# A two-layer diffusion block in split fp32: one modulation unit on VectorE, hi and lo side by side in layer 1, the last norm's shift as two columns

## The chip, the cores and the metric

The kernel runs on one core of one Trainium2 chip. The metric is the device time in microseconds of one execution, the median over runs.

## What is computed

256 context tokens and 256 tokens of x, 1024 channels each, pass through two layers; the result is the final norm of the x tokens. Each layer has a mixer (layer 0 an mLSTM in two directions, layer 1 attention over a neighbourhood and the context) and a convolutional feed-forward. Both are wrapped in a norm that is scaled and shifted, and gated, by a modulation computed from a vector (c for x, c_ctx for the context):

```python
mod_x = jnp.split((silu_c @ ada_w[i] + ada_b[i])[:, None, :], 6, axis=-1)
hx = modulate(rmsnorm(xx, norm1_g[i]), mod_x[0], mod_x[1])
yc, yx = mlstm_mixer(...)          # layer 0
yc, yx = na_mixer(...)             # layer 1, x only
xx = xx + mod_x[2] * yx
hx = modulate(rmsnorm(xx, norm2_g[i]), mod_x[3], mod_x[4])
xx = xx + mod_x[5] * conv_ffn(hx, ...)
# layer 0: the same for the context, with mod_c

def conv_ffn(h, w_up, b_up, conv_w, conv_b, w_down, b_down):
    u = dwconv(h @ w_up + b_up, conv_w, conv_b)
    a, g = jnp.split(u, 2, axis=-1)
    return (a * jax.nn.silu(g)) @ w_down + b_down
```

FF_HIDDEN is 2816, so the up product has 44 tiles of 128 rows, 22 for a and 22 for g; the down product takes 22 hidden tiles.

## The kernel before

**Numbers.** All large products keep fp32 accuracy with three matmuls of a faster kind: `split` and `split_w` (line 480s) write hi (a cast on ScalarE) and lo (the rest, a subtraction on VectorE) of a tile, and `mm3` adds hi x hi, hi x lo and lo x hi into one PSUM bank. Where one stream of 256 tokens is the moving operand (layer 1's feed-forward, the attention's output), `two_parts` already places hi and lo in the two halves of one page of 128x512.

**Storage.** 62 pages of 128x512, eight half pages, three raw weight buffers of 128x1024, five buffers each for the weights' hi and lo, eight PSUM banks.

**Order.** No engine's order is written out. The functions record operations into a `Plan`; its `run` schedules the list once, with a cost for each operation, into one fixed sequence for each engine. Among the operations that could start on an engine it takes the one that is due first. An operation is due when its earliest TensorE user needs it, with TensorE's own recorded order as the clock (`nominal`), but at most `LATE` (1,000,000 ns, so in effect never) after its nominal time. All instructions are issued from one line of `run`, L141; the profile therefore tells them apart by tile names.

**Modulation.** Twelve units (layer, u), u = 0 to 5: u = 0, 1 and 3, 4 hold halves of shift and scale of the two norms, u = 2 and 5 the two gates. (0, 0) and (0, 1) come first in a special form. The others are emitted one step at a time by `trickle()`, called after tiles of the main work; `ada_need` finishes a unit where it is needed. `ada_tensor` (tiles `ra`, `ada`, `adat`) does a unit with 2 x 32 small matmuls and two transposes. `ada_vector` does it on VectorE: for each of eight row blocks m it loads two pages, and one `scalar_tensor_tensor` per page and stream multiplies by the row `crow` and sums along it (written to `aj` for the context's stream and over `ra` itself for x's). `ADA_VECTOR` lists the units done so: (0, 4) and all of layer 1. Layer 1's later units are needed for x alone.

```python
ADA_VECTOR = [(0, 4)] + [(1, u) for u in range(6)]
```

**The feed-forward of layer 0** (`feed_forward(0)`, 512 tokens) goes in three groups of hidden tiles (8, 8, 6): all up tiles of the group, then eight down tiles `dn` (weights `rdn`, `hdn`, `ldn`), each followed by `residual`. In the first group ScalarE first copies the bank to a half page `rb` with the bias, and VectorE adds gate x `rb` to the token page `xr`. Gate 2, unit (0, 5), is due just ahead of these. An up tile (`up`, in `ffn_up`) is 8 x `mm3`; ScalarE then reads the bank twice, once for `fu` (with bias) and once for `fc`; VectorE adds the two outer taps to `fc`; ScalarE makes `sg`, VectorE the product `pr`, and `split` the hidden pair (`hhid`, `lhid`, or `bhid` side by side in layer 1).

**Layer 1** after its attention: `no`, eight output tiles from the pages `boS`, each with `residual` (through `rb`) and `norm_add`. Then `last_feed_forward` on x's 256 tokens: up tiles of j and, four tiles behind (`LAG`), the down products of an earlier j, into four banks. The first up tiles don't wait for the norm: `Early` multiplies the tokens by the norm's scale (`etn`), splits them (`ben`), and starts the products of four up tiles `ms` from them, with weights `ren21up` loaded in half pages by `paged_w`; the norm's factor comes in afterwards, as `mup` = bank x `rsn`. The shift's part of these four tiles is made apart by `shift_terms`: 32 small fp32 matmuls `wsn<-ren21up,shn` on TensorE, a copy `wssn`, a transpose, a copy `wsen`. `norm_end` makes the factor: `rbn<-ones,sqn`, `msn`, a power on GpSimd `rsn`, the diagonals `dhn` and `dln`, `rbn<-dhn`. The remaining tiles use the normed pages `bhn`.

Of the kernel before, what the change touches and what calls it, by code (L numbers as in the profile page):

```python
# [9 lines left out]
F32 = mybir.dt.float32  # L10
# [48 lines left out]
ADA_VECTOR = [(0, 4)] + [(1, u) for u in range(6)]  # L59
# [3 lines left out]
class Plan:  # L63
# [13 lines left out]
    SWITCH = 1300  # L77
    PATIENCE = 2500
# [8 lines left out]
    def __init__(self, nc, tc):  # L87
# [7 lines left out]
        self.slow = set()  # L95
        self.ops_engine = []
# [87 lines left out]
    def add(self, engine, cost, ins, outs, fns, table, dma=False):  # L184
# [30 lines left out]
        self.ops.append(dict(i=i, e=engine, frees=any(x.space == bass.MemoryType.PSUM for x in ins), window=self.AHEAD_LOAD if load else self.AHEAD_PAGE if takes else self.AHEAD, cost=cost, deps=deps, tiles=tiles, fns=fns, table=table,  # L215
# [3 lines left out]
    def run(self):  # L219
# [17 lines left out]
        for o in reversed(ops):  # L237
# [6 lines left out]
            due[o["i"]] = min(t, nominal[o["i"]] + self.LATE)  # L244
# [159 lines left out]
def diffusion_block(ctx: ExitStack, tc: tile.TileContext, I: dict, out: bass.AP):  # L404
# [92 lines left out]

    def two_parts(name, n):
# [112 lines left out]
    def ada_vector(l, u):  # L611
# [100 lines left out]
    def shift_terms(name, raw, shift, streams):  # L712
# [15 lines left out]
        return e  # L728

# [477 lines left out]
    def ffn_up(l, streams, early, ms, h):  # L1207
# [7 lines left out]
        def up(j, part):  # L1215
# [15 lines left out]
            else:  # L1231
                ps = bank(f"up{l}{m}")
                W = split_w(I["ff_up"][l, m], f"up{l}{m}")
                for k in range(KD):
                    mm3(ps[:, :n], cut(W, P * k, P * k + P), cut(h[k], 0, n), k == 0, k == KD - 1)
                nc.scalar.activation(out=u[:, :n], in_=ps[:, :n], func=AF.Identity, bias=V("fbu", 44 * l + m), scale=1.0)
                nc.scalar.activation(out=acc[:, :n], in_=ps[:, :n], func=AF.Identity,
                                     scale=V("fcw", 132 * l + 44 + m), bias=cb2[:, m:m + 1])
# [442 lines left out]
```

## Time and profile before

| | |
|---|---|
| median of 3 runs | 1173.64 us (1173.47 to 1176.03) |
| profiled execution | 1174.22 us |
| its span, first to last instruction | 1172.4 us |
| granted TensorE clock, mean | 0.998 |
| TensorE busy | 1151.6 us, 98% |
| weight loads busy (beside TensorE) | 964.6 us, 82% |
| VectorE busy | 919.8 us, 78% |
| ScalarE busy | 697.8 us, 60% |
| GpSimd busy | 26.3 us, 2% |

Times on the page are microseconds unless marked ns. An engine's busy share is an average over stages with different limits; the table of windows splits it. The chain of waits follows the work that ended last back to the start, and so says whose time the span is made of. A duration in a timeline reaches to the end of an instruction's effect, and instructions on one engine overlap: the price of a repeated one is read from start to start, or from a piece of the chain divided by its count. In order of time the stages are: the first norm and the modulation's start to 50 us, the mLSTM to about 400, layer 0's feed-forward to 783, layer 1's products and attention to 944, its output to 970, the last norm to 990, the last feed-forward to the end.

### The profile page before, as it was taken

To read this page: it belongs to the slowest core of one execution; us is meant where nothing else is said; L and a number is where in the kernel's file an instruction comes from. 1 tells how busy PE (TensorE), PEld (TensorE's weight loads), DVE (VectorE), ACT (ScalarE), POOL (GpSimd) and SP (SyncE) were. 2 spreads that over 40 slices of the span, in tenths; PEclk is the share of its full clock that TensorE was granted. 3 is DMA by queue.
4 is the path that set the end of the run, shared out by engine and by line. 5 is a ranking of instruction groups with operands and counts; after the bars stand their busy time and mean duration, and the time that the engine had idled before them with its cause. 6 is when DMAs were issued, how large, how long until landed. Compare 5 with 4: busy or idle time off the path is not lost.

```text
span 1172.4 us, 18464 instructions
## 1 busy us (share of the span) xinstructions
PE 1151.6 (98%) x6760; PEld 964.6 (82%) x6760; DVE 919.8 (78%) x1967; ACT 697.8 (60%) x1263; POOL 26.3 (2%) x57
## 2 busy tenths in 40 slices
PE   7999999999999999999999999999999999999997
PEld 5777788888888788888888888888888788999996
DVE  4999777887797689875887557788688879958776
ACT  5675665663665448542555234565678877857663
POOL 0000000010000000000000000001000000000000
PEclk9999999999999999999999999999999999999999
DMA  9955226323247223444444444543643553676652
GB/s 340 357 205 195 87 103 233 108 67 105 73 142 255 88 56 116 129 159 143 131 156 136 164 141 143 199 142 95 214 136 117 168 158 107 188 221 204 199 181 71
DMA packets 74283, 182.65 MB, mean 156 GB/s; under 512 B 9680, under 2 KB 12240, under 8 KB 74192
## 3 DMA queue, kind: packets, MB, share of 16 engines
q1 hardware_dynamic: 74192, 181.47, 47.6%
q8 instruction: 53, 0.87, 0.3%
q14 instruction: 38, 0.31, 0.1%
HBM read 177.23 MB, written 4.20 MB: 155 GB/s over the span
## 4 chain that ended last, share of the span: by engine, by line
PE 85%; DVE 4%; DMA 4%; ACT 4%; issue 1%; POOL 0%; SPq 0%; POOLq 0%; ACTq 0%; DVEq 0%
PE up L141 30%; PE dn L141 15%; PE z L141 8%; PE wo L141 6%; PE u L141 5%; PE va L141 4%; PE sc L141 3%; PE h L141 3%; PE k L141 2%; DMA aq<-in_ada0c 2%; PE q L141 2%; DMA ah<-in_ada0h 1%; PE v L141 1%; PE s L141 1%; PE o L141 1%
## 5 line engine op out<-in xcount | busy, mean ns | idle before, releaser
L141 ACT CAST hup<-rup 128x1024 fp32r<-128x1024 f32 x80 | 83.9, 1051 | 110.5 <-PE up L141 51.3
L141 DVE TENSOR_TENSOR lup<-rup,hup 128x1024 fp32r<-128x1024 f32 x80 | 97.6, 1224 | 45.0 <-ACT hup L141 44.8
L141 PE MATMUL up<-hhn,hup 128*128 128x512 f32 x320 | 124.5, 389 | 0.0
L141 PE MATMUL up<-lhn,hup 128*128 128x512 f32 x320 | 124.5, 389 | 0.0
L141 PE MATMUL up<-hhn,lup 128*128 128x512 f32 x320 | 124.5, 389 | 0.0
L141 PE MATMUL up<-bhn,hup 128*128 128x256 f32 x640 | 116.6, 284 | 0.5 <-ACT xt L141 0.2
L141 DVE SCALAR_TENSOR_TENSOR fc<-fu,vec,fc 128x510 f32<-128x510 f32 (+1 forms) x176 | 106.2, 614 | 1.7
L141 PEld LDWEIGHTS up<-bhn,hup 128*128 128x128 f32 x640 | 101.0, 192 | 2.4 <-ACT xt L141 0.4
L141 PE MATMUL up<-bhn,lup 128*128 128x256 f32 x320 | 90.5, 283 | 0.0
L141 DVE SCALAR_TENSOR_TENSOR ra<-ra,crow 128x512 f32<-128x512 f32 x112 | 76.7, 687 | 11.1 <-DMA ra<-in_adav 10.0
L141 DVE TENSOR_TENSOR ldn<-rdn,hdn 128x1024 fp32r<-128x1024 f32 (+1 forms) x46 | 54.1, 1178 | 27.9 <-ACT hdn L141 27.9
L141 ACT CAST hdn<-rdn 128x1024 fp32r<-128x1024 f32 (+1 forms) x46 | 46.4, 1011 | 46.9 <-PE up L141 26.5
L141 PEld LDWEIGHTS up<-hhn,lup 128*128 128x128 f32 x320 | 60.1, 188 | 12.6
L141 PEld LDWEIGHTS up<-hhn,hup 128*128 128x128 f32 x320 | 60.1, 188 | 12.5
L141 PEld LDWEIGHTS up<-lhn,hup 128*128 128x128 f32 x320 | 60.1, 188 | 12.4
L141 PE MATMUL dn<-lhid,hdn 128*128 128x512 f32 x176 | 68.6, 390 | 0.0
L141 PE MATMUL dn<-hhid,hdn 128*128 128x512 f32 x176 | 68.5, 389 | 0.0
L141 PE MATMUL dn<-hhid,ldn 128*128 128x512 f32 x176 | 68.5, 389 | 0.0
L141 PEld LDWEIGHTS up<-bhn,lup 128*128 128x128 f32 x320 | 61.3, 192 | 0.0
L141 PE MATMUL dn<-hdn,bhid 128*128 128x512 f32 x176 | 57.4, 390 | 0.0
L141 ACT ACTIVATE fc<-up,cb,vec 128x512 f32<-128x512 f32 (+1 forms) x80 | 53.1, 664 | 0.0
L141 PE MATMUL z<-hhn,hw 128*128 128x512 f32 x128 | 51.3, 401 | 0.0
(365 smaller groups left out, 3034.8 us busy)
## 6 DMA issues: line engine op xcount, KB each, us to landing
rup<-in_ff_up SPq DMA_DIRECT2D x80, 512.0 KB, 3.7
ra<-in_adav SPq DMA_DIRECT2D x112, 256.0 KB, 3.9
rw<-in_w_in SPq DMA_DIRECT2D x28, 512.0 KB, 5.6
ra<-in_ada SPq DMA_DIRECT2D x48, 256.0 KB, 5.2
rdn<-in_ff_last SPq DMA_DIRECT2D x22, 512.0 KB, 3.8
rwo<-in_w_out SPq DMA_DIRECT2D x16, 512.0 KB, 5.0
rdn<-in_ff_down SPq DMA_DIRECT2D x16, 512.0 KB, 3.7
aq<-in_ada0c SPq DMA_DIRECT2D x16, 256.0 KB, 5.4
```

Source lines behind the costliest of these rows:

```text
L141: fn = lambda: getattr(getattr(self.nc, engine), method)(*args, **kw)
```

## The change

It has four parts.

1. Unit (0, 5), gate 2, joins `ADA_VECTOR`.
2. `mm2` takes a moving page with hi and lo side by side (`both`): one matmul of 512 columns for hi x (hi, lo) into both halves of the bank, and one of 256 for lo x hi into the first half, where `mm3` had three of 256. It is used in layer 1's up tiles (not the early ones) and in `no`. The two halves of the bank are added afterwards: ScalarE writes the first half with the bias, VectorE adds the second, and `fc` (or the residual) is made from that.
3. `EarlyOne` replaces `Early` at the last norm. Two more up tiles are early, six in all, weights come through the raw buffers (`split_w`), and the shift is two more columns of the moving page (258 wide, `hen`, `len`), so that the shift's part is in the same bank; `shift_terms` is gone there.
4. Layer 1's modulation slices are due at most `STEADY` = 40000 ns after their nominal time, instead of `LATE`.

```diff
-ADA_VECTOR = [(0, 4)] + [(1, u) for u in range(6)]
+ADA_VECTOR = [(0, 4), (0, 5)] + [(1, u) for u in range(6)]
...
+    STEADY = 40000
...
-            due[o["i"]] = min(t, nominal[o["i"]] + self.LATE)
+            due[o["i"]] = min(t, nominal[o["i"]] + o["late"])
...
+    def mm2(ps, a, page2, start, stop):
+
+        with nc.group():
+            if not start:
+                nc.tensor.matmul(ps[:, :S], a[1], page2[:, :S], start=False, stop=False)
+            nc.tensor.matmul(ps, a[0], page2, start=start, stop=stop)
+            if start:
+                nc.tensor.matmul(ps[:, :S], a[1], page2[:, :S], start=False, stop=False)
...
+                    nc.late = nc.STEADY if l else nc.LATE
                     nc.vector.scalar_tensor_tensor(out=junk, in0=w, scalar=1.0, in1=crow[s, i], op0=ALU.mult, op1=ALU.mult,
                                                    accum_out=acc[:, i, m, s:s + 1])
+                    nc.late = nc.LATE
...
+    class EarlyOne:
...
+            N = S + 2
+            ws = [split_w(w, f"e{name}{x}") for w, x in zip(srcs[:2], labels)]
+            A = norm_scale(l, which, s, name)
+            e, self.t = [], []
+            for k in range(KD):
+                t = page(f"et{name}{k}")
+                nc.vector.tensor_copy(out=t[:, S:N], in_=mpair[l][which][:, 0, k, s:s + 1].broadcast_to([P, 2]))
+                nc.scalar.activation(out=t[:, :S], in_=X[k][:, S * s:S * s + S], func=AF.Copy, scale=A[:, k:k + 1])
+                e.append(split(t[:, :N], f"e{name}{k}", N))
+                self.t.append(t)
...
+                    mm3(self.ps[i][:, :N], cut(ws[i], P * k, P * k + P), cut(e[k], 0, N), k == 0, k == KD - 1)
...
+            nc.vector.tensor_copy(out=self.terms[:, i], in_=self.ps[i][:, S:S + 2])
...
+                if n == S:
+                    for k in range(KD):
+                        mm2(ps, cut(W, P * k, P * k + P), both(h[k]), k == 0, k == KD - 1)
+                    nc.scalar.activation(out=u[:, :n], in_=ps[:, :S], func=AF.Identity, bias=V("fbu", 44 * l + m),
+                                         scale=1.0)
+                    nc.vector.tensor_tensor(out=u[:, :n], in0=u[:, :n], in1=ps[:, S:], op=ALU.add)
+                    nc.scalar.activation(out=acc[:, :n], in_=u[:, :n], func=AF.Identity,
+                                         scale=V("fcw", 132 * l + 44 + m), bias=V("fcb", 44 * l + m))
...
-            mm3(ps[:, :S], cut(W, P * k, P * k + P), cut(O[k], 0, S), k == 0, k == KD - 1)
-        residual(n, ps[:, :S], mgate[1][0], 1, V("bo", n))
+            mm2(ps, cut(W, P * k, P * k + P), both(O[k]), k == 0, k == KD - 1)
+        b = half_page(f"no{n}")
+        nc.scalar.activation(out=b, in_=ps[:, :S], func=AF.Identity, bias=V("bo", n), scale=1.0)
+        nc.vector.tensor_tensor(out=b, in0=b, in1=ps[:, S:], op=ALU.add)
+        residual(n, b, mgate[1][0], 1)
...
-        ms = [0, KF, 1, KF + 1]
-        early = Early(l, 1, [1], name, [I["ff_up"][l, m] for m in ms], [(0, S)] * 4, [f"up{l}{m}" for m in ms])
+        ms = [0, KF, 1, KF + 1, 2, KF + 2]
+        early = EarlyOne(l, 1, 1, name, [I["ff_up"][l, m] for m in ms], [f"up{l}{m}" for m in ms])
```

Counted over the whole program, PE has 32 matmuls `ada` fewer and no `wsn<-ren21up`; 640 + 320 up matmuls of 256 columns on `bhn` become 304 of 512 and 304 of 256; the early ones go from 96 to 144. VectorE has 192 instructions with `crow` instead of 160, 38 adds `fu<-fu,up` and eight adds `no<-no,no` of 256 columns more. Loads of modulation pages stay as many.

The scheduler moves instructions accordingly; three places follow.

VectorE, in the first group of layer 0's feed-forward, after the split of the first down tile's weights (`ldn`). Before:

```order
L141 SCALAR_TENSOR_TENSOR aj_1214,aa_1079<-ra_1213,crow_546 128x512
L141 SCALAR_TENSOR_TENSOR fc_1288<-fu_1287,vec,fc_1288 128x2x255
L141 SCALAR_TENSOR_TENSOR ra_1213,aa_1079<-ra_1213,crow_548 128x512
L141 SCALAR_TENSOR_TENSOR fc_1288<-fu_1287,vec,fc_1288 128x2x255
L141 TENSOR_TENSOR pr_1296<-fc_1280,sg_1295 128x512
L141 TENSOR_TENSOR ldn_1350<-rdn_1348,hdn_1349 128x1024
L141 SCALAR_TENSOR_TENSOR aj_1226,aa_1079<-ra_1225,crow_545 128x512
L141 SCALAR_TENSOR_TENSOR fc_1300<-fu_1299,vec,fc_1300 128x2x255
L141 TENSOR_TENSOR lhid_1298<-pr_1296,hhid_1297 128x512
```

Now, at the same place of the same engine:

```order
L143 SCALAR_TENSOR_TENSOR fc_1286<-fu_1285,vec,fc_1286 128x2x255
L143 SCALAR_TENSOR_TENSOR ra_1271,aa_1222<-ra_1271,crow_548 128x512
L143 SCALAR_TENSOR_TENSOR fc_1286<-fu_1285,vec,fc_1286 128x2x255
L143 SCALAR_TENSOR_TENSOR aj_1284,aa_1222<-ra_1283,crow_545 128x512
L143 SCALAR_TENSOR_TENSOR aj_1292,aa_1222<-ra_1291,crow_546 128x512
L143 TENSOR_TENSOR pr_1294<-fc_1278,sg_1293 128x512
L143 SCALAR_TENSOR_TENSOR ra_1283,aa_1222<-ra_1283,crow_547 128x512
L143 TENSOR_TENSOR ldn_1347<-rdn_1345,hdn_1346 128x1024
L143 SCALAR_TENSOR_TENSOR fc_1298<-fu_1297,vec,fc_1298 128x2x255
L143 TENSOR_TENSOR lhid_1296<-pr_1294,hhid_1295 128x512
L143 SCALAR_TENSOR_TENSOR fc_1298<-fu_1297,vec,fc_1298 128x2x255
```

The slices (with `crow`) stand closer: four between the first two `ldn` where there were two.

VectorE around the last `no` tiles (`lno`, `no`: the attention's output; `xr` its residual adds; `len21up`, `ben` or `len`: the early products' weights and tokens). Before:

```order
L141 SCALAR_TENSOR_TENSOR xr_555<-rb_2387,mg_101,xr_555 128x256
L141 SCALAR_TENSOR_TENSOR xr_556<-rb_2393,mg_101,xr_556 128x256
L141 TENSOR_TENSOR len21up_2416<-ren21up_2413,hen21up_2415 128x512
L141 TENSOR_TENSOR ben_2435<-etn_2434,ben_2435 128x256
L141 TENSOR_TENSOR ben_2437<-etn_2436,ben_2437 128x256
L141 SCALAR_TENSOR_TENSOR ra_1722,aa_1661<-ra_1722,crow_547 128x512
L141 SCALAR_TENSOR_TENSOR xr_557<-rb_2399,mg_101,xr_557 128x256
L141 TENSOR_TENSOR ben_2439<-etn_2438,ben_2439 128x256
```

Now, at the same place of the same engine:

```order
L143 TENSOR_TENSOR no_2407<-no_2407,no_2403 128x256
L143 SCALAR_TENSOR_TENSOR xr_552<-no_2383,mg_101,xr_552 128x256
L143 SCALAR_TENSOR_TENSOR xr_553<-no_2389,mg_101,xr_553 128x256
L143 SCALAR_TENSOR_TENSOR xr_554<-no_2395,mg_101,xr_554 128x256
L143 SCALAR_TENSOR_TENSOR xr_555<-no_2401,mg_101,xr_555 128x256
L143 SCALAR_TENSOR_TENSOR xr_556<-no_2407,mg_101,xr_556 128x256
L143 TENSOR_TENSOR no_2413<-no_2413,no_2409 128x256
L143 TENSOR_TENSOR len21up_2429<-ren21up_2427,hen21up_2428 128x1024
L143 TENSOR_TENSOR len_2436<-etn_2434,hen_2435 128x258
L143 SCALAR_TENSOR_TENSOR xr_557<-no_2413,mg_101,xr_557 128x256
```

The adds of the bank's second half stand ahead of the residual adds, and no slice with `crow` is left here.

TensorE after the last `no` tile. Before, with the shift's small matmuls and their transpose:

```order
L141 MATMUL no_2407<-boS_2319,lno_2410 128x256
L141 MATMUL no_2407<-boS_2364,hno_2409 128x256 x2
L141 MATMUL no_2407<-boS_2364,lno_2410 128x256
L141 MATMUL wsn_2430<-ren21up_2413,shn_2429 32x128
...
L141 MATMUL up_2450<-ben_2435,len21up_2416 128x256
L141 MATMUL up_2450<-ben_2437,hen21up_2415 128x256 x2
L141 MATMUL up_2450<-ben_2437,len21up_2416 128x256
L141 MATMUL up_2450<-ben_2439,hen21up_2415 128x256 x2
L141 MATMUL up_2450<-ben_2439,len21up_2416 128x256
L141 MATMUL wsn_2430<-con,wssn_2431 128x128
L141 MATMUL up_2450<-ben_2441,hen21up_2415 128x256 x2
```

Now, at the same place of the same engine:

```order
L143 MATMUL no_2421<-boS_2378,lno_2424 128x256
L143 MATMUL no_2421<-boS_2378,hno_2423 128x512
L143 MATMUL up_2458<-hen_2435,hen21up_2428 128x258
L143 MATMUL up_2458<-len_2436,hen21up_2428 128x258
L143 MATMUL up_2458<-hen_2435,len21up_2429 128x258
L143 MATMUL up_2458<-hen_2438,hen21up_2428 128x258
L143 MATMUL up_2458<-len_2439,hen21up_2428 128x258
L143 MATMUL up_2458<-hen_2438,len21up_2429 128x258
L143 MATMUL up_2458<-hen_2441,hen21up_2428 128x258
```

The early products begin right behind the last `no` matmul, with `hen`, `len` and 258 columns.

## Rows read from the trace of the kernel before

**Rows 1.** The page: busy time of each engine, and the chain's shares

```profile
PE 1151.6 (98%) x6760; PEld 964.6 (82%) x6760; DVE 919.8 (78%) x1967; ACT 697.8 (60%) x1263; POOL 26.3 (2%) x57
...
PE 85%; DVE 4%; DMA 4%; ACT 4%; issue 1%; POOL 0%; SPq 0%; POOLq 0%; ACTq 0%; DVEq 0%
```

**Rows 2.** The table of windows, six stretches of the program (first line: columns)

```profile
core 0: us, PE busy (x) PEld busy (x) DVE busy (x) ACT busy (x) POOL busy (x), PEclk, DMA share, GB/s
434.00:511.00 77.00, 77.00 (x344) 63.78 (x344) 70.62 (x124) 50.06 (x85) 2.33 (x3) 1.00 0.41 127
...
783.00:826.00 43.00, 42.69 (x272) 35.98 (x272) 37.01 (x82) 25.14 (x44) 3.93 (x8) 1.00 0.43 136
900.00:944.00 44.00, 42.72 (x315) 34.40 (x314) 37.31 (x119) 36.88 (x90) 0.00 (x0) 1.00 0.54 170
970.00:990.00 20.00, 18.25 (x192) 17.00 (x184) 19.30 (x51) 13.69 (x28) 1.86 (x1) 1.00 0.34 107
1006.00:1151.00 145.00, 145.00 (x1026) 136.60 (x1025) 110.55 (x170) 95.08 (x162) 0.00 (x0) 1.00 0.66 196
```

**Rows 3.** The chain of waits: start us, us, engine and line, matmuls

```profile
370.28 1.86 PE ada L141 x32
...
554.64 87.04 PE up L141 x384
...
1119.72 5.75 PE up L141 x48
```

**Rows 4.** The timeline of PE, last norm: start us, us, operation, [idle before <-releaser]

```profile
969.80 1.95 PE L141 MATMUL wsn<-ren21up,shn 128*32 128x128 f32 x64
...
973.68 0.33 PE L141 MATMUL wsn<-con,wssn 128*128 128x128 f32 x1 [0.65 <-DVE wssn L141]
973.76 0.48 PE L141 MATMUL up<-ben,hen21up 128*128 128x256 f32 x2
...
985.82 1.47 PE L141 MATMUL xt<-con,xr 128*128 128x128 f32 x12
```

**Rows 5.** VectorE's groups, whole span: busy us, mean ns | idle us before

```profile
L141 DVE SCALAR_TENSOR_TENSOR ra<-ra,crow 128x512 f32<-128x512 f32 x112 | 76.7, 687 | 11.1 <-DMA ra<-in_adav 10.0
```

**Rows 6.** The timeline of VectorE, first feed-forward, first group of hidden tiles

```profile
433.84 0.16 DVE L141 TENSOR_SCALAR msn<-rbn 128x2 f32<-128x2 f32 x1 [3.29 <-PE rbn L141]
...
438.75 1.90 DVE L141 TENSOR_TENSOR etn<-etn,rsn 128x512 f32<-128x512 f32 x3 [0.18 <-ACT rsn L141]
...
477.15 0.68 DVE L141 SCALAR_TENSOR_TENSOR aj<-ra,crow 128x512 f32<-128x512 f32 x1
...
479.38 1.22 DVE L141 TENSOR_TENSOR lup<-rup,hup 128x1024 fp32r<-128x1024 f32 x1 [0.81 <-ACT hup L141]
...
490.26 1.23 DVE L141 TENSOR_TENSOR ldn<-rdn,hdn 128x1024 fp32r<-128x1024 f32 x1 [1.07 <-ACT hdn L141]
491.40 0.68 DVE L141 SCALAR_TENSOR_TENSOR aj<-ra,crow 128x512 f32<-128x512 f32 x1
...
492.01 0.74 DVE L141 SCALAR_TENSOR_TENSOR fc<-fu,vec,fc 128x510 f32<-128x510 f32 x1
...
517.76 0.69 DVE L141 SCALAR_TENSOR_TENSOR aj<-ra,crow 128x512 f32<-128x512 f32 x1 [0.52 <-DMA ra<-in_adav]
...
518.37 0.69 DVE L141 TENSOR_TENSOR lhid<-pr,hhid 128x512 fp32r<-128x512 f32 x1
```

**Rows 7.** VectorE's groups between 805 and 990 us

```profile
L141 DVE SCALAR_TENSOR_TENSOR ra<-ra,crow 128x512 f32<-128x512 f32 x27 | 18.3, 684 | 0.8 <-DMA ra<-in_adav 0.6
```

**Rows 8.** The timeline of PE, first down product

```profile
519.34 0.39 PE L141 MATMUL dn<-lhid,hdn 128*128 128x512 f32 x1
```

**Rows 9.** PE's waits: what was waited for: us, times, longest

```profile
PE o L141 <- ACT ptS L141: 0.9, 3, 0.3
```

**Rows 10.** The timeline of VectorE, start of the last feed-forward

```profile
991.64 1.09 DVE L141 TENSOR_TENSOR mup<-up,rsn 128x256 f32<-128x256 f32 x3
```

**Rows 11.** The timeline of VectorE, first down product's residual adds

```profile
551.24 0.88 DVE L141 SCALAR_TENSOR_TENSOR xr<-rb,mg,xr 128x256 f32<-128x256 f32 x2
```

More of the change, by code (lines that the diff above doesn't have):

```diff
@@ L95, in __init__ @@
         self.slow = set()
+        self.late = self.LATE
         self.ops_engine = []
@@ L214, in add @@
         load = dma and outs[0].space != bass.MemoryType.DRAM
-        self.ops.append(dict(i=i, e=engine, frees=any(x.space == bass.MemoryType.PSUM for x in ins), window=self.AHEAD_LOAD if load else self.AHEAD_PAGE if takes else self.AHEAD, cost=cost, deps=deps, tiles=tiles, fns=fns, table=table,
+        self.ops.append(dict(i=i, e=engine, frees=any(x.space == bass.MemoryType.PSUM for x in ins), window=self.AHEAD_LOAD if load else self.AHEAD_PAGE if takes else self.AHEAD, cost=cost, deps=deps, tiles=tiles, fns=fns, table=table, late=self.late,
                              outs=outs, dma=dma, slow=dma and any(x.tensor.name in self.slow for x in ins + outs), load=dma and outs[0].space != bass.MemoryType.DRAM))
@@ L496, in mm3, with both @@
             nc.tensor.matmul(ps, a[1], b[0], start=False, stop=stop)
+    def mm2(ps, a, page2, start, stop):
[5 more added lines that the diff above has]
+                nc.tensor.matmul(ps[:, :S], a[1], page2[:, :S], start=False, stop=False)
+    def both(b):
+        assert b[0].tensor.name == b[1].tensor.name and b[1].offset == b[0].offset + S
+        return bass.AP(b[0].tensor, b[0].offset, [list(b[0].ap[0]), [1, 2 * S]])
     def two_parts(name, n):
@@ L728, in shift_terms, with __init__, part, take @@
         return e
+    class EarlyOne:
+        def __init__(self, l, which, s, name, srcs, labels):
+            N = S + 2
[8 more added lines that the diff above has]
+                self.t.append(t)
+            self.ps = [bank(f"{x}") for x in labels]
+            self.cols, self.streams = [(0, S)] * len(srcs), [s]
+            def part(i, ks):
+                for k in ks:
+                    mm3(self.ps[i][:, :N], cut(ws[i], P * k, P * k + P), cut(e[k], 0, N), k == 0, k == KD - 1)
+            for ks in (range(KD - 1), (KD - 1,)):
+                for i in range(2):
+                    part(i, ks)
+            self.rb = page(f"rs{name}")
+            nc.scalar.copy(out=self.rb[:, :S], in_=norm_end(name, s))
+            for i in range(2, len(srcs)):
+                ws.append(split_w(srcs[i], f"e{name}{labels[i]}"))
+                part(i, range(KD))
+            self.terms = nc.tile(sm, [P, 8, 2], F32, f"wst{name}", "wst", 1)
+        def take(self, i, name):
+            q = page("m" + name)
+            nc.vector.tensor_tensor(out=q[:, :S], in0=self.ps[i][:, :S], in1=self.rb[:, :S], op=ALU.mult)
+            nc.vector.tensor_copy(out=self.terms[:, i], in_=self.ps[i][:, S:S + 2])
+            return q
     class Early:
@@ L1233, in up @@
                 W = split_w(I["ff_up"][l, m], f"up{l}{m}")
[L1234 to L1238, printed above, removed]
+                if n == S:
[6 more added lines that the diff above has]
+                                         scale=V("fcw", 132 * l + 44 + m), bias=V("fcb", 44 * l + m))
+                else:
+                    for k in range(KD):
+                        mm3(ps[:, :n], cut(W, P * k, P * k + P), cut(h[k], 0, n), k == 0, k == KD - 1)
+                    nc.scalar.activation(out=u[:, :n], in_=ps[:, :n], func=AF.Identity, bias=V("fbu", 44 * l + m),
+                                         scale=1.0)
+                    nc.scalar.activation(out=acc[:, :n], in_=ps[:, :n], func=AF.Identity,
+                                         scale=V("fcw", 132 * l + 44 + m), bias=cb2[:, m:m + 1])
             conv_taps(acc, u, ns, (-1, 1), lambda j: V("fcw", 132 * l + 44 * (j + 1) + m))
```

## The prediction

> **What bounds the kernel now.** I read the page's engine shares first: TensorE (PE) is busy 98% of the span and holds 85% of the chain of waits that ends last, VectorE (DVE) 78%, ScalarE 60% [rows 1]. So the time is the sum of TensorE's matmuls, and an edit pays what it takes off PE, unless something makes PE wait. The table of windows shows where that could happen: in the first feed-forward's first group of eight hidden tiles (434 to 511 us) VectorE is busy 70.62 of 77 us, while PE runs without a gap; around the last norm (970 to 990) VectorE is busy 19.30 of 20 and PE loses 1.75 us; in the last feed-forward (1006 to 1151) PE is full and VectorE has 34 us free [rows 2]. Third, the chain gives the price of a matmul where PE never waits: 384 up matmuls of 512 columns in 87.04 us, 226.7 ns each; 48 of 256 columns in 5.75 us, 119.8 ns each [rows 3]. From these two, a column costs (226.7 - 119.8)/256 = 0.418 ns, and each matmul some 12.9 ns besides (119.8 - 256 x 0.418). The granted clock is 1.00 in each window quoted, that is 2.4 GHz, so no term here is a matter of the clock.
>
> **The change part by part, on PE.**
> Gate 2 leaves TensorE: two halves of 32 matmuls, 1.86 us each (the first stands in [rows 3], the second at 395.85 reads alike), and two transposes at 0.12 us (twelve such in 1.47 us [rows 4]): -3.96 us.
> Hi and lo side by side in layer 1's up products: 38 tiles x 8 steps = 304 times, two matmuls of 256 columns (239.6 ns) become one of 512 (226.7 ns), 12.9 ns each: -3.92 us. In the attention's output product 64 times: -0.83 us. Here the row stands against a rule. The Trainium skill, "TensorE: Matmul & The Clock Gate", section "Back-to-back issue gap", puts the spacing of an isolated matmul at N/2.4 + 2.5 ns; by it a merge would save only 2.5 ns, 0.9 us in all instead of 4.75. The measured 119.8 ns is for matmuls in a stream with a weight load each, and I take the row.
> The shift's own products of the last norm go: 1.95 us of small matmuls, a transpose (0.08 us from its start to the next one's), and PE's 0.65 us wait for their copy [rows 4]: -2.68 us. In their place 144 matmuls are two columns wider: 144 x 2 x 0.418 ns = +0.12 us.
> Sum on PE: -3.96 - 3.92 - 0.83 - 2.68 + 0.12 = **-11.27 us**.
>
> **What VectorE gets for it.** Gate 2 brings 32 more multiply-and-sum instructions over a 128x512 page, while its 16 loads of a page on the SP queue take the place of 16 others. One takes 687 ns [rows 5]; where another kind follows, the next starts 0.61 us after it (491.40 to 492.01 [rows 6]). Even spreading moves layer 1's slices too: by the order, the whole rest of the modulation now stands ahead of the attention, where 27 of them ran between 805 and 990 us before [rows 7].
> First place: the first feed-forward. From the norm's statistics at 433.84 to the last hidden split at 518.37 the trace has 17 such instructions (477.15 the first, 517.76 the last), and no idle at all from 438.8 to 479.4; after that twelve waits, 0.81 us the first, 0.52 us the last, which add to 8.1 us [rows 6]. PE takes that last split at 519.34, 0.3 us after it is ready at 519.06 [rows 6, 8]. The order puts 33 there: 16 x 0.61 to 0.69 = 9.8 to 11.1 us more, less 1.1 us for one weight split that moves ahead of the norm. So 8.7 to 10.0 us of new work meet 8.1 us of idle, 0.3 of slack and some 0.7 us by which PE itself comes there later (a small piece stands elsewhere in its order). If all idle fills, nothing is lost; if none does, 8.9 us. The waits are on ScalarE's casts and a load, which a VectorE that runs late finds done, so it lies near the lower end: I take a quarter of the idle as staying, **+2.0** (0 to 8.9). Late next are the first down product's matmuls on the eighth hidden tile, and behind them the rest of the group.
> Second place: the first norm of layer 1 (783 to 826), seven more of them, 4.5 us, into 6.0 us of VectorE idle [rows 2]: **+0.5** (0 to 4.5).
> Third: the attention, from which they go. PE's gaps in 900 to 944 are 1.28 us, most of it on ScalarE's copies of the transposed softmax [rows 2, 9], and a slice in VectorE's order holds up what stands behind it by 0.6 us; I take **-0.5** (-1.3 to 0).
> Fourth: the last norm. VectorE is nearly full there, so its ledger decides whether the 2.68 us are kept. It loses two modulation slices and the two copies of the shift's products, gains eight adds of half a page for the output product and eight copies of two columns for the shift; an add from PSUM starts 0.34 us after the one before (three in 1.09 us [rows 10]), so the adds are 2.7 us, most of them ahead of 970. PE has two more early products (48 matmuls, 5.8 us) to do while the norm is finished: they cover the rest of PE's 1.75 us of gaps there (1.1 without the copy's wait), and draw two weight splits of 1.2 us forward. **0** (-1.1 to +2.7).
> Fifth: the last feed-forward's adds. Some 34 in 1006 to 1151, 34 x 0.34 = 11.6 us; VectorE then has 122.2 us of work in about 141.5 us of PE time: **0**. ScalarE's second pass over each tile now reads SBUF, off the path.
> The last 21 us, after the final up product, have only what they had: 0. The DMA queues carry as many loads as before, at a share of 0.41 in the first place [rows 2]: 0.
>
> Sum: -11.27 + 2.0 + 0.5 - 0.5 = **-9.3 us**. The profiled execution took 1174.22 us (span 1172.4 and 1.8 outside), 0.58 above the runs' median of 1173.64; so 1174.22 - 9.27 = 1164.95 for such an execution and **1164.4** for the median. A measurement of this kernel can tell 0.2%, 2.35 us, from no change.
>
> **The rivals.**
> (1) VectorE absorbs everything: all idle fills, both +2.0 and +0.5 fall away and the attention's gaps close by 1.3. Time -12.57: 1161.1. For it: VectorE's total only rises from 78% to about 82%. Against: the fill has to be complete to a tenth in the first feed-forward. 0.17.
> (2) The merge saves nothing, a matmul's time being its columns alone and the 12.9 ns something else of these two stages: 4.75 comes back, 1169.2. Against: the two rows of the chain, both in gapless stretches [rows 3]. 0.08. The Trainium skill's rule named above would give almost this, 1168.2 by its 2.5 ns a pair.
> (3) Half the idle of the first feed-forward stays: 0.9 + 4.05 = 5.0 there, and 2.0 at layer 1's first norm: 1168.9. For it: the same ScalarE queue feeds these waits, 1.07 us ahead of the first down split [rows 6]. 0.14.
> (4) None of it fills: 8.9 and 2.0, so -9.27 + 8.4 = -0.9, 1172.8: no change that can be told. The gate's last slices also stand ahead of the first residual add, which ran at 551.24 [rows 11], by the order three weight splits earlier now, so the half pages would add to it. 0.07.
> (5) Slower: in the last feed-forward each new add waits, in VectorE's fixed order, for ScalarE's pass over the same bank, which waits for PE; the taps and splits queued behind it wait too, and PE waits for the hidden splits. VectorE has 141.5 - 122.2 = 19.3 us over for 34 adds, so a wait of 0.57 us each makes it the bound, and above (19.3 + 11.6)/34 = 0.91 us each the kernel is slower by over 0.2%. At the longest wait of this kind in the rows, 1.07 us [rows 6], it is 36.4 - 19.3 = 17.1 us: 1181.5. Against: the order sets ScalarE's pass well ahead, and with four tiles of lag the hidden splits have a down product's time to spare. 0.06.
>
> **How the numbers follow.** Forecast 0.48, rivals 0.17, 0.08, 0.14, 0.07 and 0.06 in turn. The range goes from rival 1 to a little above rival 3: 1161.0 to 1170.0, which leaves out rivals 4 and 5 and a tail of the others, nearly 2 in 10. Faster by over 0.2% (below 1171.3): 0.48 + 0.17 + 0.08 + 0.14 = 0.87; within: 0.07; slower: 0.06.
>
> **What would show it.** In the chain, two up tiles of the last feed-forward take 16 x (226.7 + 119.8) ns = 5.54 us where 5.75 stood; if 5.7, rival 2. No piece of 1.95 us of shift products and no wait behind them. 64 modulation matmuls (as the profile counts them) fewer on PE. VectorE without idle from 438 to about 518, and a wait of PE for the last hidden split near 519 of 0 (rival 1), about 2 (forecast), 5 (rival 3) or more. No modulation slices after 805, and fewer waits in 900 to 944. In the last feed-forward, PE without gaps and the adds' wait under 0.57 us; if not, rival 5. The prediction is wrong in its reasons if the time falls by this much while PE waits appear elsewhere and one of the three matmul terms is missing.

## The result, and the profile after

The changed kernel takes 1167.19 us (median of 4 runs, 1167.05 to 1169.91) against 1174.12 for the kernel before on the same chip (1173.47 to 1176.03): a ratio of 0.9944, 95% interval 0.9931 to 0.9957, 6.9 us less. The forecast was 9.3 us less. The profiled execution took 1167.05 us, with a span of 1165.3.

The page after, engines and the chain's shares, for [rows 1]:

```profile
PE 1142.3 (98%) x6261; PEld 943.5 (81%) x6261; DVE 951.3 (82%) x2091; ACT 698.9 (60%) x1259; POOL 26.2 (2%) x56
...
PE 79%; DVE 9%; DMA 5%; ACT 4%; issue 2%; SPq 0%; POOL 0%; POOLq 0%; DVEq 0%; ACTq 0%
```

VectorE has 31 us more work, TensorE nine less. The chain is PE's for 79% where it was 85%, and VectorE's for 9% where it was 4%.

The table of windows after, with the columns of [rows 2] (us, PE, weight loads, VectorE, ScalarE, GpSimd, clock, DMA share, GB/s). The first four stretches answer to four of those rows, the last three cut the last feed-forward:

```profile
430.00:508.00 78.00, 78.00 (x351) 64.60 (x350) 76.38 (x146) 51.08 (x85) 2.59 (x3) 1.00 0.44 142
781.00:823.00 42.00, 41.95 (x269) 35.68 (x269) 39.52 (x94) 24.83 (x43) 4.82 (x10) 1.00 0.33 108
897.00:941.00 44.00, 43.66 (x321) 36.55 (x320) 35.99 (x121) 36.89 (x90) 0.00 (x0) 1.00 0.32 100
965.00:985.00 20.00, 19.73 (x161) 19.35 (x160) 19.11 (x48) 16.86 (x33) 1.53 (x1) 1.00 0.55 176
1000.00:1040.00 40.00, 40.00 (x214) 34.30 (x214) 39.15 (x74) 31.55 (x55) 0.00 (x0) 1.00 0.74 203
1040.00:1062.00 22.00, 19.42 (x97) 16.30 (x96) 11.58 (x20) 10.78 (x19) 0.00 (x0) 0.92 0.68 171
1062.00:1144.00 82.00, 82.00 (x437) 70.31 (x436) 72.00 (x120) 55.81 (x93) 0.00 (x0) 1.00 0.66 204
```

In the first feed-forward's first group (430 to 508) VectorE is now busy 76.38 of 78 us, and PE still all 78. The idle of [rows 6] lay between 438 and 518, and there it is filled:

```profile
438.00:518.00 80.00, 80.00 (x355) 66.25 (x354) 79.70 (x154) 51.76 (x87) 0.00 (x0) 1.00 0.47 152
```

PE lost nothing by it. In the attention's 44 us PE's gaps are 0.34 us where [rows 2] had 1.28. The one stretch that is worse than any of before is 1040 to 1062, where PE is busy 19.42 of 22 us and the granted clock is 0.92. Some of PE's waits after (us in total, times, longest); the first one shown was not there before:

```profile
...
PE up L143 <- ACT xt L143: 2.6, 1, 2.6
...
PE v L143 <- DVE lq L143: 1.6, 3, 0.8
...
PE o L143 <- ACT ptS L143: 0.7, 2, 0.3
...
PE rbn L143 <- DVE dhn L143: 0.3, 1, 0.3
PE dn L143 <- DVE lhid L143: 0.2, 1, 0.2
```

Where the time went, stage by stage. The starts of PE's first or last matmul of a kind are read from its timeline in both profiled executions; the forecast's terms are put to the stage that they belong to. Each column is one execution: over the ten profiled executions of this document that have the gate on VectorE, the first line alone runs from 417.2 to 419.1.

| stage, from PE's | before, us | after, us | measured | forecast |
|---|---|---|---|---|
| start to first early up product of layer 0 | 421.79 | 418.95 | -2.8 | -4.0 |
| to layer 1's first key product | 363.46 | 363.93 | +0.5 | +2.0 |
| to its first value product | 18.90 | 18.66 | -0.2 | +0.5 |
| to the last `no` product | 165.45 | 164.22 | -1.2 | -1.3 |
| to the first product on `bhn` | 17.86 | 19.83 | +2.0 | +2.8 |
| to the last one | 163.23 | 157.92 | -5.3 | -9.2 |
| to the end | 21.76 | 21.76 | 0.0 | 0.0 |

In the fifth line the forecast holds two more early products (5.79 us) and their extra columns (0.12), less the shift's 2.68 and less four transposes that stand elsewhere now (4 x 0.12); the sixth has the other side of both. The second, third and fifth stage did better than forecast by 3.0 us together, the first 1.2 us worse, and the last feed-forward 3.9 us worse. What that stage loses goes at one place. PE's timeline after:

```profile
1050.13 0.60 PE L143 MATMUL xt<-con,xr 128*128 128x128 f32 x4
1053.30 0.50 PE L143 MATMUL up<-bhn,hup 128*128 128x512 f32 x1 [2.58 <-ACT xt L143]
...
1054.65 0.63 PE L143 MATMUL up<-bhn,hup 128*128 128x512 f32 x1
1055.08 0.41 PE L143 MATMUL up<-bhn,lup 128*128 128x256 f32 x1
...
1058.24 0.40 PE L143 MATMUL up<-bhn,hup 128*128 128x512 f32 x1
1058.47 0.28 PE L143 MATMUL up<-bhn,lup 128*128 128x256 f32 x1
```

PE waits 2.58 us for `xt`, ScalarE's copy of a transposed bank. Soon after it goes on, its matmuls slow down: the 512-column matmul at 1054.65 takes 0.43 us to the next start, the one at 1058.24 takes 0.23. The granted clock (third figure from the end) in between is about half:

```profile
1054.60:1058.00 3.40, 3.40 (x12) 2.81 (x11) 2.53 (x5) 3.40 (x7) 0.00 (x0) 0.52 0.56 154
```

That is the lower level, 1.2 GHz, where the rest of the stage has 2.4, for some 3 us behind the wait. The starts of all matmuls from 1050 to 1075, less their usual spacing, leave about 4.5 us: 2.7 around the wait, 1.7 for the slow matmuls. All four executions of the changed kernel have a mean clock of 0.995 or 0.996 (0.998 in the profile before). ScalarE's timeline tells why `xt` was late:

```profile
1042.14 0.60 ACT L143 ACTIVATE fc<-fu,vec 128x256 f32<-128x256 f32 x1
1051.72 1.04 ACT L143 CAST hup<-rup 128x1024 fp32r<-128x1024 f32 x1 [8.98 <-DMA rup<-in_ff_up]
1052.67 0.58 ACT L143 COPY xt<-xt 128x512 f32<-128x512 f32 x1
```

ScalarE stood 8.98 us, at the head of its queue a weight cast (`hup`) whose load had not landed. The copy of `xt` behind it needed nothing from that load. The queue of SP, and the chain at that place:

```profile
1035.73 0.38 SPq L143 DMA_DIRECT2D gd<-gs  x1
1036.16 0.57 SPq L143 DMA_DIRECT2D brow<-in_rows  x1
1036.78 0.82 SPq L143 DMA_DIRECT2D frow<-in_rows  x1
1037.70 0.38 SPq L143 DMA_DIRECT2D rup<-in_ff_up  x1
```

```profile
1037.70 13.94 DMA rup<-in_ff_up
...
1121.69 5.59 PE up L143 x32
```

The load issued at 1037.70 took 13.94 us, where such loads took 3.7 us in the median before. Ahead of it stands `gd<-gs`, the write of gate 5's row to memory: 4 KB, with a transposed pattern. The DMA's GB/s in 40 slices of 0.5 us from 1034, after:

```profile
GB/s 238 418 189 115 197 352 271 148 39 33 33 12 29 20 45 37 49 33 53 12 29 29 33 16 16 61 193 188 303 401 373 426 426 418 418 385 381 160 41 20
```

From 1038 to 1046 they moved 12 to 53 GB/s; of the 2164 packets from 1034 to 1054, 1167 have under 512 bytes. Later, with loads alone, it is over 400. The kernel before does the same write; its GB/s from 1019, and ScalarE's two waits for loads behind it:

```profile
GB/s 287 344 131 131 123 262 304 196 104 96 78 57 53 29 16 29 8 12 20 25 25 25 20 4 37 139 307 311 324 311 385 426 418 418 393 307 291 135 29 66
```

```profile
1028.86 1.05 ACT L141 CAST hup<-rup 128x1024 fp32r<-128x1024 f32 x1 [4.04 <-DMA rup<-in_ff_up]
...
1035.62 1.05 ACT L141 CAST hdn<-rdn 128x1024 fp32r<-128x1024 f32 x1 [3.68 <-DMA rdn<-in_ff_last]
```

There ScalarE waits 4.04 and 3.68 us, but PE waits for nothing: its weights are ready 8 to 9 us ahead of their use just then, 5 to 12 us from the stage's first tile to the write, and 2.9 at the least behind it (end of VectorE's split to PE's first use, from the timelines). In the changed kernel that lead begins at 4.0 us, falls to 0.1 at the fifth tile, and has come to 7.5 when the write comes. The six early products' weights hold the three raw buffers at the stage's start, which may be why; the run with pages below doesn't bear that out. So there were two theories: the row's transfers, the write above all (A), or the lead (B).

### The profile page after: what moved, and what is told of

Same layout as the page of the kernel before. It is cut to its first block, busy times and chain, and to the rows that moved or that the text cites. A ratio compares the mean times of both kernels' runs of the same rounds, so it can differ in the third digit from the quotient of the medians.

```text
span 1165.3 us, 17598 instructions
## 1 busy us (share of the span) xinstructions
PE 1142.3 (98%) x6261; PEld 943.5 (81%) x6261; DVE 951.3 (82%) x2091; ACT 698.9 (60%) x1259; POOL 26.2 (2%) x56
## 4 chain that ended last, share of the span: by engine, by line
PE 79%; DVE 9%; DMA 5%; ACT 4%; issue 2%; SPq 0%; POOL 0%; POOLq 0%; DVEq 0%; ACTq 0%
PE up L143 26%; PE dn L143 11%; PE u L143 7%; PE z L143 7%; PE wo L143 6%; PE va L143 4%; PE k L143 3%; DMA rup<-in_ff_up 3%; PE h L143 3%; PE sc L143 3%; PE q L143 2%; PE s L143 1%; PE o L143 1%; PE v L143 1%; DVE lup L143 1%
## 5 line engine op out<-in xcount | busy, mean ns | idle before, releaser
L143 DVE TENSOR_TENSOR lup<-rup,hup 128x1024 fp32r<-128x1024 f32 x78 | 95.2, 1222 | 36.6 <-ACT hup L143 36.0
L143 PE MATMUL up<-bhn,hup 128*128 128x512 f32 x304 | 108.3, 401 | 2.6 <-ACT xt L143 2.6
L143 DVE SCALAR_TENSOR_TENSOR ra<-ra,crow 128x512 f32<-128x512 f32 x128 | 86.3, 686 | 4.4 <-DMA ra<-in_adav 3.9
L143 PE MATMUL up<-bhn,lup 128*128 128x256 f32 x304 | 79.5, 281 | 0.0
L143 PEld LDWEIGHTS up<-bhn,hup 128*128 128x128 f32 x304 | 56.5, 190 | 14.1 <-ACT xt L143 2.8
L143 PEld LDWEIGHTS up<-bhn,lup 128*128 128x128 f32 x304 | 58.0, 191 | 3.3 <-DVE lup L143 0.3
L143 ACT ACTIVATE sg<-fc 128x512 f32<-128x512 f32 (+1 forms) x44 | 23.0, 523 | 58.7 <-DVE fc L143 58.6
```

The costliest lines, as they stand in the source:

```text
L143: fn = lambda: getattr(getattr(self.nc, engine), method)(*args, **kw)
```

## The experiments

Each ratio is to the kernel before, run on the same chip. The runs below come from three chips, on which the kernel before took 1174.1, 1174.4 and 1174.6 us, so that a difference between runs of two chips is uncertain by up to half a microsecond from this alone.

**The rows ahead.** The write of the row and the loads of `grow`, `brow` and `frow` are asked for in the attention, behind head pair 4; nothing else of the last feed-forward is touched. The modulation slices stay where they were (the last at 789.4 us in the changed kernel, 787.1 here).

```diff
     for m in range(KD):
...
         attend(m, pn)
+        if m == 4:
+            last_rows()
...
+    def last_rows():
+        l = 1
+        ada_need(1, 5)
+        nc.late = 0
+        gd = dr.tile([KD, P], F32, name="gd")
...
+        nc.late = nc.LATE
...
-            if j == 5:
-                ada_need(l, 5)
...
-                nc.sync.dma_start(out=gd.rearrange("k p -> p k"), in_=gs)
```

> The changed kernel with one thing moved: the write of gate 5's row to memory in pieces of four bytes (gd<-gs) and the loads of the rows (grow, brow, frow) stand in the attention instead of in the last feed-forward. Theory A: the changed kernel loses 2.6 us of PE waiting near 1050 us and some 2 us more of matmuls at the lower granted clock right behind it, because a weight load took 13.9 us beside that write, ScalarE's cast of it stood at the head of its queue, and the bank copy behind the cast came late. Then this run is about 4.7 us faster than the changed kernel: ratio to before 0.990, 1162.4 us. Theory B: the weights of the last feed-forward have no lead in the changed kernel (0.1 to 4 us at its start, against 5 to 12 before), since the early products' weights use the three raw buffers; the row write only shows it, and the stall comes elsewhere: under 1.5 us faster, 1165.7 or more.

Measured: 1162.23 us, ratio 0.9896 (0.9882 to 0.9909), 5.0 us faster than the changed kernel. Its chain at the same place, and the first feed-forward's first group in its table of windows:

```profile
1040.29 5.57 PE up L143 x32
1045.86 2.73 PE dn L143 x12
1048.59 0.44 PE xt L143 x4
...
434.00:507.00 73.00, 73.00 (x324) 60.50 (x324) 72.93 (x139) 49.34 (x84) 0.00 (x0) 1.00 0.45 146
```

The tiles follow each other without a wait. The lead at the stage's start is as thin as in the changed kernel (4.0 falling to 0.1 us), so theory A is borne out and B is not needed. The move takes the write and the rows' loads together, but in this run they land 35 us apart, and the trace tells which of them slows the loads. The write is issued at 817.08, alone, and the weight load behind it (`rk`, 512 KB) took 12.1 us; `brow` and `grow` are issued from 852.5 on, among weight loads of 3.7 and 3.4 us (KB, then us to landing, in the DMA view's windows 818 to 819 and 852 to 858):

```profile
817.08 0.38 SPq L143 DMA_DIRECT2D gd<-gs  x1
818.21 0.33 SPq L143 DMA_DIRECT2D rk<-in_w_qk  x1
```

```profile
rk<-in_w_qk SPq DMA_DIRECT2D x1, 512.0 KB, 12.1
```

```profile
rq<-in_w_qk SPq DMA_DIRECT2D x1, 512.0 KB, 3.7
brow<-in_rows SPq DMA_DIRECT2D x2, 256.0 KB, 4.3
grow<-gd SPq DMA_DIRECT2D x2, 256.0 KB, 4.8
rk<-in_w_qk SPq DMA_DIRECT2D x1, 512.0 KB, 3.4
```

So the write is enough by itself, and the rows' loads without it slow nothing. PE loses nothing by the write here: from 815 to 835 it is busy 20.00 of 20 us. From PE's first product on `bhn` to the last it is 153.7 us, 9.5 less than before, where the forecast had 9.2. This version beats both kernels.

**The weights through pages.**

```diff
-            ws = [split_w(w, f"e{name}{x}") for w, x in zip(srcs[:2], labels)]
+            ws = [paged_w(w, f"e{name}{x}")[0] for w, x in zip(srcs[:2], labels)]
...
-                ws.append(split_w(srcs[i], f"e{name}{labels[i]}"))
+                ws.append(paged_w(srcs[i], f"e{name}{labels[i]}")[0])
```

> The changed kernel with the six early products' weights loaded through pages again (two halves each), which leaves the three raw buffers to the last feed-forward. Theory A: the slow write still falls on a weight load, so the stall near 1050 stays for the most part unless there is lead: 0 to 2 us faster than the changed kernel's 1167.1. Theory B: with lead of 5 us or more the slow load is covered: about 4.7 us faster, 1162.4.

Measured: 1164.48 us, ratio 0.9916 (0.9903 to 0.9930), 2.7 us faster than the changed kernel, 2.3 slower than with the rows ahead. The chain has the write's victim again, and PE's waits another waiter:

```profile
1039.80 13.30 DMA rdn<-in_ff_last
```

```profile
PE up L143 <- DVE fu L143: 2.9, 1, 2.9
```

Now it is a load of a down tile (`rdn`) that takes 13.3 us; ScalarE's cast of it holds up `fu`, and VectorE's add on `fu` the bank. The weights were 8.0 us ahead here, and PE waited 2.9 us all the same: what waits is not the weight's user but whatever stands behind the cast on ScalarE. The lead at the stage's start wasn't raised by the pages either (5.7 falling to 0.1), so the raw buffers alone don't make it thin; what does stays open. The difference to the changed kernel has another part: behind this wait, longer than that of 2.58 us, the clock did not fall,

```profile
1049.00:1062.00 13.00, 10.13 (x56) 8.42 (x55) 6.82 (x12) 6.54 (x12) 0.00 (x0) 1.00 0.69 242
```

and the mean clock is 0.999 in all four executions. Why it fell in the one and not in the other is not shown.

**The kernel before, rows ahead.** The same move in the old kernel.

```diff
+    def last_rows():
...
+        if m == 4:
+            last_rows()
...
-            if j == 5:
-                ada_need(l, 5)
...
```

> The kernel before, with the write of gate 5's row and the loads of the rows moved into the attention, and nothing else. Theory A (the write slows whatever load is under way, and is hidden in the kernel before by weights that are ready 8 to 9 us ahead): within 0.5 us of the kernel before, 1173.6 to 1174.6. Rival: the write cost the kernel before as much as the changed one, and the move is a gain of its own of about 4.9 us: 1169.

Measured: 1174.77 us, ratio 1.0002 (0.9994 to 1.0011): the same. In its profile the last feed-forward takes 163.3 us, as before, so the write cost the old kernel nothing there. The move also asked for unit (1, 5) early, and the stretch from the first value product to the last score took 1.2 us more than in the kernel before (141.1 and 139.9); that belongs to the move and not to the write.

**Rows ahead and pages.** Both edits together.

```diff
+            last_rows()
...
+            ws = [paged_w(w, f"e{name}{x}")[0] for w, x in zip(srcs[:2], labels)]
```

> As the run with the rows ahead, with the early products' weights through pages. If lead at the start of the last feed-forward is worth something by itself (PE waits 0.3 us there in the run with the rows ahead): at most 0.5 us faster. If not: the same, 1162.2 within 0.5; the pages' sixteen half loads and four more splits could cost 0.5 to 1.

Measured: 1162.45 us, ratio 0.9896 (0.9883 to 0.9910): the same as with the rows ahead alone. The lead at the start is as thin with pages (5.8 falling to 0.1 us), so this run doesn't tell what more lead would be worth; it does tell that pages or raw buffers make no difference that can be measured.

**Three matmuls again,** beside the rows ahead; VectorE's 46 adds of the two halves go with it.

```diff
-                        mm2(ps, cut(W, P * k, P * k + P), both(h[k]), k == 0, k == KD - 1)
+                    mm3(ps[:, :n], cut(W, P * k, P * k + P), cut(h[k], 0, n), k == 0, k == KD - 1)
...
-            mm2(ps, cut(W, P * k, P * k + P), both(O[k]), k == 0, k == KD - 1)
+            mm3(ps[:, :S], cut(W, P * k, P * k + P), cut(O[k], 0, S), k == 0, k == KD - 1)
...
```

> As the run with the rows ahead, and with three matmuls of 256 columns again in layer 1's up tiles and in the attention's output. The price in the prediction (12.9 ns for each of 368 merges): 4.75 us slower than the run with the rows ahead. If a merge saves nothing, no slower. If VectorE's 46 adds cost PE something, between the two or faster.

Measured: 1166.01 us, ratio 0.9927 (0.9913 to 0.9940), 3.8 us slower. A pair of up tiles in its chain, for the 5.59 us of the changed kernel's:

```profile
1119.68 5.75 PE up L143 x48
```

0.16 us for each pair of tiles, 10 ns a merge where the forecast had 12.9, and by the medians 3.8 of 4.75 us. A cost of columns alone (rival 2) is out.

**Gate 2 on TensorE again,** beside the rows ahead.

```diff
-ADA_VECTOR = [(0, 4), (0, 5)] + [(1, u) for u in range(6)]
+ADA_VECTOR = [(0, 4)] + [(1, u) for u in range(6)]
```

> As the run with the rows ahead, and with gate 2 on TensorE again. If VectorE takes gate 2 for nothing: 3.96 us slower than the run with the rows ahead. The prediction's 2.0 us of loss in the first feed-forward: only 2 us slower. If it cost VectorE more than it saves, faster.

Measured: 1165.96 us, ratio 0.9926 (0.9914 to 0.9938), 3.7 us slower. VectorE takes the gate almost for nothing. What it costs stands ahead of the feed-forward. PE's wait for VectorE's split of the values' input, here:

```profile
PE v L143 <- DVE lq L143: 0.8, 2, 0.6
```

With the gate on VectorE it is 1.6 or 1.7 us in three waits, in all ten such profiles; with the gate on PE 0.8 in two, as in the kernel before. PE's first up product comes at 417.2 to 419.1 us in the profiled executions of the first kind (ten) and at 420.5 to 422.9 in those of the second (four): 3.2 us apart on average, where 3.96 was forecast.

**Gate 2 alone,** in the kernel before.

```diff
-ADA_VECTOR = [(0, 4)] + [(1, u) for u in range(6)]
+ADA_VECTOR = [(0, 4), (0, 5)] + [(1, u) for u in range(6)]
```

> The kernel before with gate 2 on VectorE alone. If VectorE takes the 32 slices for nothing: 3.96 us faster, 1170.4. If they push layer 1's slices later, into places where PE waits for VectorE (by the order, ten more of them in the last feed-forward): 2 us faster, 1172.4.

Measured: 1173.22 us, ratio 0.9984 (0.9975 to 0.9993): by the ratio about 1.9 us faster, half the price. Its SP queue, the chain and PE's timeline:

```profile
1050.60 0.48 SPq L141 DMA_DIRECT2D gd<-gs  x1
```

```profile
1052.75 13.38 DMA rup<-in_ff_up
```

```profile
1068.14 0.50 PE L141 MATMUL up<-bhn,hup 128*128 128x256 f32 x2 [1.49 <-ACT fc L141]
```

The write has moved to 1050.60 (1020.96 in the kernel before), the weight load issued behind it takes 13.38 us, ScalarE waits 9.87 us for it with a cast at the head of its queue, and PE waits 1.49 us for ScalarE's `fc` 17.5 us after the write, the only wait of that size in the last feed-forward. From the first product on `bhn` to the last it takes 165.2 us where the kernel before takes 163.2. So most of what the gate gave was lost here, with the write ahead as in the changed kernel; another 0.8 us went at the last norm (18.7 and 17.9), where PE's wait for `wssn` grew from 0.65 to 1.49 us. Nine slices run after 990 us, where the kernel before has none, and gate 5's row waits for its own.

**The spreading alone,** in the kernel before.

```diff
+    STEADY = 40000
...
+                    nc.late = nc.STEADY if l else nc.LATE
...
+                    nc.late = nc.LATE
```

> The kernel before with the even spreading of layer 1's modulation slices alone. By the prediction's terms it gains 0.5 us in the attention and loses 0.5 at layer 1's first norm: 1174.4 within 0.5. If the 27 slices that leave the attention were what held PE there: 1.5 to 2.5 us faster, 1172 to 1173.

Measured: 1172.55 us, ratio 0.9985 (0.9976 to 0.9993): 1.8 us faster. The attention from first value product to last score takes 138.1 us (139.9 before), but that score stands earlier among the output products now: to the last `no` product it is 164.9 and 165.4, a gain of 0.6, as the forecast's -0.5 for the attention has it. The last norm's stretch takes 16.6 (17.9 before), without the two slices that stood in it; that 1.3 is the larger part. At layer 1's first norm, where the forecast had +0.5, nothing changed (18.9 and 18.9).

**The spreading undone** in the changed kernel, rows where they were; and, ahead of it, beside the rows ahead.

```diff
-                    nc.late = nc.STEADY if l else nc.LATE
+                    nc.late = nc.LATE
```

> As the run with the rows ahead, with layer 1's modulation slices due as late as they may be again. If the slices that left the attention are what shortened it (from 158.6 us between the first key product and the last score in the kernel before to 156.7 in the changed one): up to 1.9 us slower, 1164.1. By the prediction's terms (0.5 gained there, 0.5 lost at layer 1's first norm): the same. If the early slices cost the first feed-forward: faster.

Measured: 1166.36 us, ratio 0.9932 (0.9918 to 0.9946), 4.1 slower than with the rows ahead. That is not the spreading's worth: the move asks for gate 5 in mid-attention, and without the spreading 16 slices come at once there. VectorE's slices between 805 and 990, 37 where [rows 7] had 27:

```profile
L143 DVE SCALAR_TENSOR_TENSOR ra<-ra,crow 128x512 f32<-128x512 f32 x37 | 24.7, 686 | 0.2
```

> The changed kernel with layer 1's slices due as late as they may be again, the rows' write where it was. (In the run with the rows ahead, the move asks for the last unit in the middle of the attention, and 16 slices came there at once, so that its 4.1 us were not the spreading's alone.) If the spreading is worth what the attention's length says, 1.5 to 2 us: 1168.9. If nothing: 1167.1. If the slices that then fall into the last feed-forward add to its stall: up to 1171.

Measured: 1171.84 us, ratio 0.9971 (0.9960 to 0.9983), 4.7 us slower than the changed kernel (4.2, with each set against the kernel before on its own chip). The queue of SP, one of ScalarE's waits, and the end of the kernel in the table of windows:

```profile
1090.13 0.38 SPq L143 DMA_DIRECT2D gd<-gs  x1
```

```profile
1105.70 1.05 ACT L143 CAST hdn<-rdn 128x1024 fp32r<-128x1024 f32 x1 [6.75 <-DMA rdn<-in_ff_last]
```

```profile
1142.00:1171.00 29.00, 17.69 (x65) 13.08 (x63) 19.89 (x36) 12.32 (x24) 1.48 (x2) 0.78 0.23 74
```

Ten slices now run in the last feed-forward, and the write comes at 1090, 54 us later than in the changed kernel. ScalarE waits 4.66 and 6.75 us for loads behind it; from 1108 on the chain is for the most part ScalarE's and VectorE's casts, splits and adds, and the last 29 us have PE at 17.69 us and a clock of 0.78. From the last up product to the end it takes 28.5 us instead of 21.8. So the spreading's largest effect here is in the last feed-forward. How much of it is the late write and how much the ten slices' own time on VectorE was not tried apart. The stretch to the last `no` product is 164.2 us in both kernels, the last norm's 21.2 without the spreading and 19.8 with it: 1.3 again.

**Spreading by 20 us** instead of 40, beside the rows ahead.

```diff
-    STEADY = 40000
+    STEADY = 20000
```

> As the run with the rows ahead, with slices due at most 20000 ns after their nominal time instead of 40000, so that the eight slices still in the attention stand ahead of it, and more of them in the first feed-forward, where VectorE is busy 72.93 of 73 us. If VectorE has no room there: slower by about the 0.61 us of each slice that moves into that stage, 1 to 3 us. If the attention gains more than that: up to 0.5 us faster, 1161.7.

Measured: 1162.39 us, ratio 0.9893 (0.9879 to 0.9906): the same as with 40. VectorE in the first feed-forward's first group:

```profile
434.00:508.00 74.00, 74.00 (x329) 61.23 (x328) 73.76 (x143) 49.18 (x83) 1.09 (x3) 1.00 0.48 156
```

It is busy 73.76 of 74 us, and PE 74 of 74: full, and still not late.

**The old early products,** beside the rows ahead.

```diff
-        ms = [0, KF, 1, KF + 1, 2, KF + 2]
-        early = EarlyOne(l, 1, 1, name, ...)
+        ms = [0, KF, 1, KF + 1]
+        early = Early(l, 1, [1], name, ...)
```

> As the run with the rows ahead, and the last norm with four early products and the shift's own products again. By the prediction's terms (2.68 us of PE less 0.12 of columns): 2.6 us slower than the run with the rows ahead, 1164.8. If the raw buffers that the six early products take cost as much as that at the start of the last feed-forward, where the weights have 0.1 to 4 us of lead: no slower or faster.

Measured: 1165.01 us, ratio 0.9918 (0.9904 to 0.9932), 2.8 us slower (2.5, with each set against the kernel before on its own chip), as the forecast's 2.56 has it; in the two profiled executions, from the last `no` product to the last one on `bhn`, it is 175.6 and 173.8 us, a little less.

## Why the prediction was right, and where it was not

The direction and the range held; the size was 2.3 us short. That it came so near is partly luck: terms missed to both sides, and one of the prediction's own signs failed, since PE has a gap in the last feed-forward, which was to run without any.

**Matmul terms.** The up merges, the shift's products and the gate were forecast at 4.75, 2.56 and 3.96 us; undone one at a time they measured 3.8, 2.8 and 3.7. The rule of the Trainium skill ("TensorE: Matmul & The Clock Gate", "Back-to-back issue gap") that was weighed against the row would have given the first 0.9; the row decided rightly. A pair of up tiles takes 5.59 us and not 5.54.

**First place, +2.0.** Mis-sized: VectorE's idle of 8.1 us filled (0.3 us are left between 438 and 518), and the stage lost 0.27 us (89.17 to 89.44 us from the first early up product to the first down product). "A quarter of the idle as staying" was a choice with no row behind it; rival 1's condition held at this place.

**Second and third place, +0.5 and -0.5.** At layer 1's first norm nothing was lost (0.2 us less instead of 0.5 more). The attention's -0.5 was about right where the spreading stands alone (0.6 to the last `no` product); in the changed kernel that stretch is as long with the spreading as without it. It gained 1.2 there, where the forecast's attention and merge terms make 1.3, and the run with three matmuls puts some 0.75 of that on the merges; what the rest is, isn't shown.

**Fourth place, 0.** The last norm did 0.8 us better than its terms. What was mis-sized is the two slices that leave it: both runs on the spreading show 1.3 us in this stretch, and the forecast had nothing for them.

**Fifth place, 0: the step that failed.** The new adds did not make VectorE the bound (rival 5), and undone they gave nothing but the merges' price. But the last feed-forward lost 3.9 us against its forecast, by a mechanism that stood in no rival. The term that failed is the 0 for the DMA queues, which the prediction dismissed with "as many loads as before"; it counted them, and didn't ask which load stands behind which transfer, and what stands behind its cast. The change shifts the row's write, the loads and PE's use of them against each other; a 4 KB write in small packets that was free in the kernel before then costs about 2 us (gate alone) or 4.5 us (the changed kernel), by where it falls; without the spreading the end is 6.7 us longer, with ten slices there as well. Moved away it costs nothing, and the sum comes to 1162.2, 2.2 us below the forecast.

## What to carry to other kernels

In a kernel where every engine has a fixed order, ask of each transfer not only whether its own user can wait, but what else stands behind that user in its queue; a bank copy behind a late cast stalls TensorE though it needs nothing of the load. A small strided write can make the large loads behind it several times as long (here 12 to 14 us for 3.7), so put it where no load is urgent, once, rather than let a scheduler's shifts decide. When a change moves several things, sum it against stages, since terms that miss to both sides can look like a good forecast.

## What was not expected of the hardware

Around a write of 4 KB in about a thousand small packets the DMA moved only 12 to 53 GB/s for some 8 us (over 400 a little later), and the next 512 KB load took 13.9 us in the changed kernel, 13.3 in the run with the pages and 13.4 with the gate alone, where the median was 3.7. Where the write stood with no row loads near it, the load behind it still took 12.1. How the small packets hold the load up is not shown.

And a PE wait of 2.6 us cost 4.5: behind it 512-column matmuls came 0.43 us apart instead of 0.23 for some 3 us, at a granted clock of 0.52. In the run with the pages a wait of 2.9 us was followed by no such stretch. What decides between the two is not shown.
